# Seven-product pairs of a split-precision feed-forward: the seeding copy behind the previous pair's last products, the sides' sums made during the output projection, the memory statistics one tile later

## The chip, the cores and the metric

One core of one Trainium2 chip runs the whole kernel in one launch. The metric is the device time in microseconds (us), the median of several executions; lower is better.

## The reference

Two transformer blocks run one behind the other on a sequence of 512 tokens of width 1024, in float32. Only the feed-forward of the first block and the start of the second block matter here:

```python
def first_block(x, ...):
    ...
        h = h + merged @ w_out[l]
        u = rms_norm(h, norm_ffn_g[l])
        g, up = jnp.split(u @ w_gate_up[l], 2, axis=-1)
        h = h + (jax.nn.silu(g) * up) @ w_down[l]
    return rms_norm(h, norm_final_g)

def second_block(x, mem, ...):
        h = rmsnorm(x, g_mix_pre[l])
        ...
        mkv = rmsnorm(mem, g_mem[l]) @ w_mem_kv[l]
```

The hidden width of the feed-forward is 2816, 22 tiles of 128 features for the gate and 22 for the up half. `mem` has 256 rows.

## The kernel before

Activations lie feature-major: eight tiles of 128 features by 512 tokens. Float32 operands are split into a high and a low part, and a product is three matmuls (high by high, high by low, low by high), all recorded at L231. For the weights the split is ACT's cast at L358 (`whi`) and DVE's subtraction at L359 (`wlo`), into six buffers. TensorE (PE) accumulates in banks of 512 float32 per partition; a bank's tiles are called `pd`, `ps` and `po` in the profile. An ordinary tile of a product is `fm`: 24 matmuls of 512 columns.

The feed-forward of block 1 (`ffn`, called with the name f1) goes over the hidden features in three parts of 8, 7 and 7 tiles. A part computes its gate and up tiles, applies silu(gate) * up, and then runs the eight `f1_dn` tiles of the down projection over the part's features; the result is added to `h`.

Of the 22 gate/up pairs one is computed the ordinary way, and 21 by a scheme with seven products of half-size blocks in place of eight (`seven`, seven pairs per part). One pair is a 2 x 2 block product: (gate, up weights; two halves of the 1024 features) times (two halves of the features; two halves of the tokens). Each of the products is 12 matmuls of 256 columns. The moving sides `11`, `21` and `22` are slices of the normalised input u; `t1` to `t4` are sums of such slices, kept as `Yh`, `V` (features' tiles 0 and 1) and `Yl`, `K` (tiles 2 and 3). `seven_prep` makes them in four steps: each step scales two tiles on ACT, makes four sums on DVE (L428 to L431) in one buffer `M`, casts 1024 columns on ACT (L535) and subtracts 1024 on DVE (L536).

The results of pair j live in two halves of one `ps` bank (g0, c0) and in a half of the one bank `po` (g1). The halves of `po` alternate with j. Product 11 goes into g0; ACT copies g0 into g1 (the seeding copy, L457); then t3 goes into c0, t2 onto g1, 21 onto g0, t1 onto g1, 22 onto g1, t4 onto c0. ACT copies g1 out twice on the way (L463 and L466), and DVE adds c0 to these copies (L468 and L473). The order on PE is written out by hand (`self.strict` chains the matmuls), a pair's head being put ahead of the last two products of the pair before, q being the pair and last the one before it:

```python
            head(q)
            if last is not None:
                tail(last)
            mid(q)
```

So PE's order is 11(q), 22(last), t4(last), t3(q), t2(q), 21(q), t1(q). The evacuation `ev_7` stands behind `tail`: DVE multiplies g0 and g1 with the norm's row factor R (L1292, L1293), ACT takes the silu (L180), DVE multiplies the up half with R (L1295), multiplies the two (L1296), and the split L535/L536 makes the part's `Ba`/`Bb` and `Ca`/`Cb`.

A framework's scheduler sets each engine's order from the order in which the program issues and from its own estimates. `done_tile` is called behind every tile: it runs the queued `hooks` (two statistics steps of a norm: `cols`, `rows`) and counts down the entries of `self.later`, running those that reach zero. Before, the four steps of `seven_prep` stand in `later` with counts 1, 1, 2, 2, so that they are issued behind the first and second tile of f1 (the gate and up tile of the ordinary pair). `part_hook` runs ahead of part 2's down tiles and issues loading the memory (`mem_load`, tile `Y`), a change of ACT's table (L169), and `mem_stats`: the memory's split (`Yh`, `Yl`), its squares on ACT, their sums on DVE (L595) and two statistics hooks.

Of the kernel before, what the change touches and what calls it, by code (L numbers as in the profile page):

```python
# [9 lines left out]
F32R = mybir.dt.float32r  # L10
# [7 lines left out]
P = 128  # L18
# [27 lines left out]
def weight_plan():  # L46
# [51 lines left out]
    for g in range(2):  # L98
        fm("gb", w, rg(4616 + 512 * g, 512))
        fm("pb", "w_proj_b", rg(512 * g, 512), kt=4)  # L100
    fm("wo", "w_out", rg(0, D))
    ffn("f1", "w_gate_up", "w_down")
    m = "w_mem_kv_2"
    fm("mk", m, rg(0, 512))
# [17 lines left out]
    for g in range(2):  # L122
        fm("ga2", w, rg(4168 + 512 * g, 512))
        fm("ua", "w_up_a_2", rg(512 * g, 512), kt=4)
    fm("wo2", "w_out_2", rg(0, D))
    ffn("f2", "w_ffn_in_2", "w_ffn_out_2")
    return plan

# [18 lines left out]
class Build:  # L147
# [290 lines left out]
    def seven(self, name, x, pairs, evac):  # L438

        nc = self.nc

        def product(ps, b, start=False):
            hi, lo = x[b]
            kw = dict(skip_group_check=True)
            for k, (wh, wl) in enumerate(self.next_half(name)):
                self.mm(ps, wh, hi(k), start=start and k == 0, stop=False, **kw)
                self.mm(ps, wh, lo(k), start=False, stop=False, **kw)
                self.mm(ps, wl, hi(k), start=False, stop=k == 3, **kw)  # L450

        def head(q):
            b = self.bk_s()
            q["g0"], q["c0"] = b[:, 0:256], b[:, 256:512]
            q["g1"] = self.seeded[:, 256 * (q["j"] % 2):256 * (q["j"] % 2) + 256]
            product(q["g0"], "11", True)
            nc.scalar.copy(q["g1"], q["g0"])  # L457

        def mid(q):
            q["u2"], q["u4"] = self.t("s7", [P, 256], F32, bufs=2), self.t("s7b", [P, 256], F32, bufs=1)  # L460
            product(q["c0"], "t3")
            product(q["g1"], "t2")
            nc.scalar.copy(q["u2"], q["g1"])  # L463
            product(q["g0"], "21")
            product(q["g1"], "t1")
            nc.scalar.copy(q["u4"], q["g1"])  # L466
            q["lin"] = self.tmp()
            nc.vector.tensor_add(q["lin"][:, 256:512], q["u4"], q["c0"])  # L468

        def tail(q):  # L470
            product(q["g1"], "22")
            product(q["c0"], "t4")
            nc.vector.tensor_add(q["lin"][:, 0:256], q["u2"], q["c0"])  # L473
            self.done_tile(lambda: evac(q["j"], q["g0"], q["g1"], q["lin"]))

        self.strict = "start"
        last = None
        for j in pairs:
            q = dict(j=j)
# [4 lines that stand above are left out]
            last = q  # L484
        if last is not None:
            tail(last)
        self.strict = None
# [771 lines left out]
    def ffn(self, name, u, st, down_evac, part_hook=None, halves=None, x7=None):  # L1259
        nc = self.nc  # L1260
        uh, ul = u
        rh, rl = self.acc_k(uh), self.acc_k(ul)
        f0 = 0
        for p, n in enumerate(FF_PARTS):
            ah, al = self.pair_tiles("Ba", "Bb"), self.pair_tiles("Ca", "Cb")
            sil = {}

            full = slice(0, S)

            def ev_g(ps, j, w=full):  # L1270
                a = self.tmp()[:, w]
                nc.vector.tensor_mul(a, ps, st["R"][:, w])
                self.last_silu = self.act(a, a, AF.Silu).ins
                sil[j, w.start] = a

            def ev_u(ps, j, w=full):
                b = self.tmp()[:, w]
                nc.vector.tensor_mul(b, ps, st["R"][:, w])
                a = sil.pop((j, w.start))
                nc.vector.tensor_mul(a, a, b)  # L1280
                self.split_to(ah(j)[:, w], al(j)[:, w], a)

            j0 = 0
            if halves is not None and p == 0:
                j0 = NUP // 2
                self.fm_halves(name + "_up", NUP, rh, rl, lambda ps, i, w: (ev_u if i % 2 else ev_g)(ps, i // 2, w),
                               halves)
                self.strict = None

            def ev_7(j, g0, g1, lin):  # L1290
                a = self.tmp()
                nc.vector.tensor_mul(a[:, 0:256], g0, st["R"][:, 0:256])  # L1292
                nc.vector.tensor_mul(a[:, 256:512], g1, st["R"][:, 256:512])  # L1293
                self.last_silu = self.act(a, a, AF.Silu).ins
                nc.vector.tensor_mul(lin, lin, st["R"])  # L1295
                nc.vector.scalar_tensor_tensor(a, lin, -1.0, a, op0=ALU.mult, op1=ALU.mult)  # L1296
                self.split_to(ah(j), al(j), a)

            j7 = n if name not in SEVEN else min(max(SEVEN[name] - f0, j0), n)
            for j in range(j0, j7):  # L1300
                self.fm(name + "_up", rh, rl, lambda ps, j=j: ev_g(ps, j))
                self.fm(name + "_up", rh, rl, lambda ps, j=j: ev_u(ps, j))
            self.seven(name + "_7", x7, range(j7, n), ev_7)
            f0 += n
            if part_hook is not None:
                part_hook(p)
            k0 = KD - NDN if halves is not None and p == 2 else KD
            for k in range(k0):
                self.fm(name + "_dn", ah, al, lambda ps, k=k: down_evac(ps, k, p, full))
            if k0 < KD:  # L1310
                self.fm_halves(name + "_dn", NDN, ah, al, lambda ps, i, w: down_evac(ps, k0 + i, p, w))


    def block1(self):
        nc = self.nc
        x = self.x
        u = uh, ul = self.new_u()
# [28 lines left out]
        q = lambda h: qt_[:, h, :]  # L1346
# [83 lines left out]
        h = self.h = self.t("H16", [P, KD, S])  # L1430
        for k in range(0, KD, 2):
            nc.sync.dma_start(h[:, k:k + 2, :], self.ins["xT"][:, k:k + 2, :])
        u = uh, ul = self.new_u()
        acc = self.t("A", [P, S], F32, bufs=2)

        def ev_wo(ps, k):
            nc.vector.tensor_add(h[:, k, :], h[:, k, :], ps)
            self.split_to(uh[:, k, :], ul[:, k, :], h[:, k, :], self.vec("norm_ffn_g", k))
            self.sq_add(acc, h[:, k, :], k == 0)

        for k in range(KD):
            self.fm("wo", *mp["m"], lambda ps, k=k: ev_wo(ps, k))
        st, self.hooks = self.stat_hooks(acc, "f")

        nx = {}

# [11 lines left out]
        def part_hook(p):  # L1458
            if p == 2:
                self.mem_load()  # L1460
                self.load_lnexp(self.last_silu)
                self.mem_stats()

        th = [self.t(tag, [P, 2, 4, 256], F32R) for tag in ("Yh", "Yl")]
        tl = [self.t(tag, [P, 2, 4, 256], F32R) for tag in ("V8", "K8")]
        x7, steps = self.seven_prep(u, lambda k: th[k // 2][:, k % 2], lambda k: tl[k // 2][:, k % 2],
                                    lambda k: h[:, k, :], lambda k: self.vec("norm_ffn_g", k))
        self.later = [[1 + k // 2, f] for k, f in enumerate(steps)]
        self.deep = True
        self.ffn("f1", u, st, ev_dn, part_hook, x7=x7)  # L1470
        self.deep = False
        return nx
# [373 lines left out]
```

## Time and profile before

| | us |
|---|---|
| median of 3 runs | 1770.49 (1768.11 to 1770.69) |
| the profiled execution | 1770.61 |
| its span in the profile | 1768.0 |
| PE busy | 1720.7 (97%) |
| DVE busy | 1124.5 (64%) |
| ACT busy | 869.0 (49%) |
| POOL busy | 153.5 (9%) |
| share of PE in the chain that ended last | 92% |

The span runs from the first to the last instruction of the profiled execution; the execution's own time is 2.6 us longer. A timeline row reads: start in us from the span's start, duration, engine, line, operation, tile written <- tiles read, count, and in brackets the engine's idle time ahead of the row and what ended it. The end of a matmul is modelled; the spacing of the starts of neighbouring matmuls tells how long one occupies PE. `PEclk` is TensorE's granted clock as a share of the full 2.4 GHz.

### The profile page before, as it was taken

The page shows a single profiled execution, that of the slowest core. Times are in us where ns is not written, and L with a number is a line of the kernel's source. Part 1 is how long each engine was busy: PE and PEld are TensorE (multiplying, and loading weights), DVE is VectorE, ACT ScalarE, POOL GpSimd, SP SyncE. Part 2 cuts the span into 40 slices and gives each one's busy share as a digit, 9 for nine tenths or more (in the row PEclk, how much of TensorE's full clock was granted, in tenths as well). Part 3 has the DMA queues.
Part 4 walks back from the last instruction along what each step waited for, and adds up shares of the span by engine and source line. Part 5 has one row for each costly group of instructions (what it writes and reads, how often), then busy time and mean ns, then how long its engine had stood idle before and what let it go on. Part 6 is the DMA issues. An engine that isn't in the chain of part 4 may idle for free.

```text
span 1768.0 us, 25895 instructions
## 1 busy us (share of the span) xinstructions
PE 1720.7 (97%) x9601; PEld 1446.7 (82%) x9601; DVE 1124.5 (64%) x2363; ACT 869.0 (49%) x1767; POOL 153.5 (9%) x203
## 2 busy tenths in 40 slices
PE   9999999998999999999999999999999999999997
PEld 8878788886988888979989876777779988888887
DVE  5887664567765856777499964666655743344454
ACT  5755655445543534564455567644544533332331
POOL 1400011000100101000000222200000500000001
PEclk9999999998999999999999999999999999999999
DMA  5434215342654645335324211323223233333331
GB/s 181 118 95 120 72 60 162 106 155 78 157 142 120 165 127 137 86 95 179 102 72 108 72 60 59 100 93 118 71 99 120 72 94 95 89 94 94 96 113 54
DMA packets 65661, 187.04 MB, mean 106 GB/s; under 512 B 7840, under 2 KB 10440, under 8 KB 65280
## 3 DMA queue, kind: packets, MB, share of 16 engines
q1 hardware_dynamic: 59456, 174.33, 31.7%
q0 software_dynamic: 6080, 11.08, 3.8%
q8 instruction: 75, 1.23, 0.3%
q14 instruction: 50, 0.41, 0.1%
HBM read 174.87 MB, written 6.84 MB: 103 GB/s over the span
## 4 chain that ended last, share of the span: by engine, by line
PE 92%; DVE 3%; ACT 2%; issue 1%; DMA 1%; POOL 0%; SPq 0%; DVEq 0%; ACTq 0%
PE pd L231 66%; PE ps L231 6%; PE po L231 5%; PE po L795 2%; PE pd L522 2%; PE pd L524 2%; PE pd L523 2%; PE ps L572 1%; PE ps L573 1%; PE ps L785 1%; PE po L1194 1%; DVE ul L539 1%; DMA raw<-in_wts 0%; ACT po L457 0%; PE ps L1160 0%
## 5 line engine op out<-in xcount | busy, mean ns | idle before, releaser
L358 ACT CAST whi<-raw 128x512 fp32r<-128x512 f32 (+3 forms) x536 | 308.7, 582 | 521.3 <-PE pd L231 392.3
L359 DVE TENSOR_TENSOR wlo<-raw,whi 128x512 fp32r<-128x512 f32 (+3 forms) x536 | 346.3, 651 | 244.0 <-ACT whi L358 235.3
L231 PE MATMUL pd<-uh,whi 128*128 128x512 f32 (+1 forms) x1032 | 406.3, 394 | 0.0
L231 PE MATMUL pd<-uh,wlo 128*128 128x512 f32 (+1 forms) x1032 | 404.9, 393 | 0.0
L231 PE MATMUL pd<-ul,whi 128*128 128x512 f32 (+1 forms) x1032 | 404.1, 392 | 0.0
L231 PEld LDWEIGHTS pd<-uh,wlo 128*128 128x128 f32 x1032 | 194.0, 188 | 43.8 <-issue 2.0
L231 PEld LDWEIGHTS pd<-ul,whi 128*128 128x128 f32 x1032 | 193.8, 188 | 41.9 <-issue 2.4
L231 PEld LDWEIGHTS pd<-uh,whi 128*128 128x128 f32 x1032 | 194.0, 188 | 41.0 <-issue 2.5
L231 PE MATMUL pd<-Ba,whi 128*128 128x512 f32 (+1 forms) x240 | 91.6, 382 | 0.0
L231 PE MATMUL pd<-Ca,whi 128*128 128x512 f32 (+1 forms) x240 | 90.9, 379 | 0.0
L231 PE MATMUL pd<-Ba,wlo 128*128 128x512 f32 (+1 forms) x240 | 90.8, 378 | 0.0
L231 PE MATMUL pd<-Bb,whi 128*128 128x512 f32 (+1 forms) x210 | 78.3, 380 | 3.1 <-ACT Bb L535 3.1
L231 PE MATMUL pd<-Bb,wlo 128*128 128x512 f32 (+1 forms) x210 | 80.5, 383 | 0.0
L231 PE MATMUL pd<-Cb,whi 128*128 128x512 f32 (+1 forms) x210 | 80.5, 383 | 0.0
L231 PE MATMUL pd<-Yh,whi 128*128 128x512 f32 (+1 forms) x192 | 72.7, 383 | 0.9 <-DVE H L751 0.9
L231 PE MATMUL pd<-Yl,whi 128*128 128x512 f32 (+1 forms) x192 | 72.4, 377 | 0.0
L231 PE MATMUL pd<-Yh,wlo 128*128 128x512 f32 (+1 forms) x192 | 72.2, 376 | 0.0
L524 PE MATMUL pd<-whi,ul 128*128 128x260 f32 (+1 forms) x232 | 64.8, 286 | 1.5 <-DVE ul L539 1.5
L522 PE MATMUL pd<-whi,uh 128*128 128x260 f32 (+1 forms) x232 | 65.8, 288 | 0.2 <-ACT uh L180 0.2
L523 PE MATMUL pd<-wlo,uh 128*128 128x260 f32 (+1 forms) x232 | 65.2, 283 | 0.0
L231 PEld LDWEIGHTS pd<-Ba,whi 128*128 128x128 f32 x240 | 45.2, 188 | 9.5 <-DVE H L1448 0.6
L231 PEld LDWEIGHTS pd<-Ba,wlo 128*128 128x128 f32 x240 | 45.1, 188 | 9.3
(525 smaller groups left out, 3696.8 us busy)
## 6 DMA issues: line engine op xcount, KB each, us to landing
raw<-in_wts SPq DMA_DIRECT2D x218, 512.0 KB, 3.6
raw<-in_wts SPq DMA_DIRECT2D x32, 448.0 KB, 3.3
PT<-in_wts SPq DMA_DIRECT2D x42, 256.0 KB, 4.2
PT<-in_wts POOLq DMA_DIRECT2D x42, 256.0 KB, 4.7
P<-in_wts SPq DMA_DIRECT2D x21, 256.0 KB, 3.6
raw<-in_wts SPq DMA_DIRECT2D x8, 520.0 KB, 3.4
tabd<-tab SPq DMA_DIRECT2D x8, 320.0 KB, 5.8
H<-in_xT SPq DMA_DIRECT2D x8, 256.0 KB, 6.3
```

The source lines that it names most:

```text
L231: return self.pe(self.nc.tensor.matmul(*args, **kw))
L358: self.nc.scalar.copy(hi, r)
L359: self.nc.vector.tensor_sub(lo, r, hi.bitcast(F32))
L522: mm(pss[i][:, :w], xh[:, kk, sl], hi, start=(kk == 0), stop=False)
L523: mm(pss[i][:, :w], xh[:, kk, sl], lo, start=False, stop=False)
L524: mm(pss[i][:, :w], xl[:, kk, sl], hi, start=False, stop=(kk == 7))
L539: nc.vector.scalar_tensor_tensor(lo, src, g, hi.bitcast(F32), op0=ALU.mult, op1=ALU.subtract)
L572: mm(out, q, khi, start=True, stop=False)
L573: mm(out, q, klo, start=False, stop=True)
L785: nc.tensor.transpose(ps[:, kt * P:(kt + 1) * P], Pt[:, kt * P:(kt + 1) * P], self.ident)
L795: nc.tensor.matmul(o[64 * hh:64 * hh + 64, qt * P:(qt + 1) * P], v[:, kt, h * 64:(h + 1) * 64], PTs[hh][:, kt * P:(kt + 1) * P], start=(kt ...
L1194: nc.tensor.matmul(o[c][64 * hh:64 * hh + 64, kt * P:], bv[:, kt, h * 64:(h + 1) * 64], us[hh]["a"][:, :N], start=False, stop=True, skip_g ...
```

## The change

Four things are done.

1. The seeding copy moves from the end of `head` to the start of `mid`, so that it is issued behind the last two products of the pair before (it is L459 now).
2. The evacuation is cut in two. `ev_7g` (DVE's products of g0 and g1 with R, now L1294 and L1295, and the silu) is issued between products 22 and t4; `ev_7` (the up half, L1300 and L1301, and the split, now L537/L538) behind t4. `done_tile` has nothing left to evacuate.
3. `seven_prep` is called ahead of the loop over the output projection's tiles (`wo`). Steps 0 and 1 are issued behind its tiles 5 and 6; steps 2 and 3 behind the first tile of f1 (counts 0 and 0).
4. `mem_stats` leaves `part_hook` and is issued behind the first down tile of part 2.

```diff
--- before.py
+++ after.py
@@ -454,9 +454,9 @@
             q["g0"], q["c0"] = b[:, 0:256], b[:, 256:512]
             q["g1"] = self.seeded[:, 256 * (q["j"] % 2):256 * (q["j"] % 2) + 256]
             product(q["g0"], "11", True)
+
+        def mid(q):
             nc.scalar.copy(q["g1"], q["g0"])
-
-        def mid(q):
             q["u2"], q["u4"] = self.t("s7", [P, 256], F32, bufs=2), self.t("s7b", [P, 256], F32, bufs=1)
             product(q["c0"], "t3")
             product(q["g1"], "t2")
@@ -469,9 +469,11 @@
 
         def tail(q):
             product(q["g1"], "22")
+            gate = evac[0](q["g0"], q["g1"])
             product(q["c0"], "t4")
             nc.vector.tensor_add(q["lin"][:, 0:256], q["u2"], q["c0"])
-            self.done_tile(lambda: evac(q["j"], q["g0"], q["g1"], q["lin"]))
+            evac[1](q["j"], gate, q["lin"])
+            self.done_tile(lambda: None)
 
         self.strict = "start"
         last = None
@@ -1287,11 +1289,14 @@
                                halves)
                 self.strict = None
 
-            def ev_7(j, g0, g1, lin):
+            def ev_7g(g0, g1):
                 a = self.tmp()
                 nc.vector.tensor_mul(a[:, 0:256], g0, st["R"][:, 0:256])
                 nc.vector.tensor_mul(a[:, 256:512], g1, st["R"][:, 256:512])
                 self.last_silu = self.act(a, a, AF.Silu).ins
+                return a
+
+            def ev_7(j, a, lin):
                 nc.vector.tensor_mul(lin, lin, st["R"])
                 nc.vector.scalar_tensor_tensor(a, lin, -1.0, a, op0=ALU.mult, op1=ALU.mult)
                 self.split_to(ah(j), al(j), a)
@@ -1300,7 +1305,7 @@
             for j in range(j0, j7):
                 self.fm(name + "_up", rh, rl, lambda ps, j=j: ev_g(ps, j))
                 self.fm(name + "_up", rh, rl, lambda ps, j=j: ev_u(ps, j))
-            self.seven(name + "_7", x7, range(j7, n), ev_7)
+            self.seven(name + "_7", x7, range(j7, n), (ev_7g, ev_7))
             f0 += n
             if part_hook is not None:
                 part_hook(p)
@@ -1438,9 +1443,16 @@
             self.split_to(uh[:, k, :], ul[:, k, :], h[:, k, :], self.vec("norm_ffn_g", k))
             self.sq_add(acc, h[:, k, :], k == 0)
 
+        th = [self.t(tag, [P, 2, 4, 256], F32R) for tag in ("Yh", "Yl")]
+        tl = [self.t(tag, [P, 2, 4, 256], F32R) for tag in ("V8", "K8")]
+        x7, steps = self.seven_prep(u, lambda k: th[k // 2][:, k % 2], lambda k: tl[k // 2][:, k % 2],
+                                    lambda k: h[:, k, :], lambda k: self.vec("norm_ffn_g", k))
         for k in range(KD):
             self.fm("wo", *mp["m"], lambda ps, k=k: ev_wo(ps, k))
+            if k in (5, 6):
+                steps[k - 5]()
         st, self.hooks = self.stat_hooks(acc, "f")
+        self.later = [[0, steps[2]], [0, steps[3]]]
 
         nx = {}
 
@@ -1459,13 +1471,8 @@
             if p == 2:
                 self.mem_load()
                 self.load_lnexp(self.last_silu)
-                self.mem_stats()
-
-        th = [self.t(tag, [P, 2, 4, 256], F32R) for tag in ("Yh", "Yl")]
-        tl = [self.t(tag, [P, 2, 4, 256], F32R) for tag in ("V8", "K8")]
-        x7, steps = self.seven_prep(u, lambda k: th[k // 2][:, k % 2], lambda k: tl[k // 2][:, k % 2],
-                                    lambda k: h[:, k, :], lambda k: self.vec("norm_ffn_g", k))
-        self.later = [[1 + k // 2, f] for k, f in enumerate(steps)]
+                self.later = [[1, self.mem_stats]]
+
         self.deep = True
         self.ffn("f1", u, st, ev_dn, part_hook, x7=x7)
         self.deep = False
```

Three places of the order that results are shown.

ACT around the seeding copy of the second pair of part 0; `whi` are weight casts, `tmp` the silu, `s7b` the copy at L466. Before:

```order
L466 COPY s7b_4592<-po_4389 128x256
L358 CAST whi_4683<-PT_4395 128x512
L457 COPY po_4389<-ps_4665 128x256
L358 CAST whi_4709<-raw_4572 128x512
L358 CAST whi_4736<-T_4738 128x512
L180 ACTIVATE tmp_4726<-tmp_4726 128x512
L358 CAST whi_4754<-P_4397 128x512
```

With the change:

```order
L466 COPY s7b_4592<-po_4055 128x256
L358 CAST whi_4682<-PT_4417 128x512
L358 CAST whi_4712<-raw_4572 128x512
L180 ACTIVATE tmp_4698<-tmp_4698 128x512
L459 COPY po_4055<-ps_4665 128x256
L358 CAST whi_4736<-T_4738 128x512
L358 CAST whi_4754<-P_4419 128x512
```

The copy stood ahead of the cast of `raw`; it now stands behind the silu of the pair before, which stands two casts earlier than it did.

PE at the change from product t4 of the first pair (into `ps_4559`) to t3 of the second (into `ps_4665`); the bracket names the engine whose semaphore a row waits for. Before:

```order
L231 MATMUL ps_4559<-Yl_4386,whi_4611 128x256
L231 MATMUL ps_4559<-K_1023_4388,whi_4611 128x256
L231 MATMUL ps_4559<-Yl_4386,wlo_4612 128x256
L231 MATMUL ps_4665<-Yh_4385,whi_4628 128x256
L231 MATMUL ps_4665<-V_1022_4387,whi_4628 128x256
```

With the change:

```order
L231 MATMUL ps_4559<-Yl_4052,whi_4611 128x256
L231 MATMUL ps_4559<-K_965_4054,whi_4611 128x256
L231 MATMUL ps_4559<-Yl_4052,wlo_4612 128x256
L231 MATMUL ps_4665<-Yh_4051,whi_4628 128x256 [waits Activation_49]
L231 MATMUL ps_4665<-V_964_4053,whi_4628 128x256
```

The first matmul of t3 has a wait for ACT that it did not have. The instruction on ACT that it waits for is the copy L459.

ACT in the first pair of part 0, up to the last step of `seven_prep`; `R` is the norm's row factor, the casts to `Yl` belong to steps 2 and 3. Before:

```order
L642 COPY R_4527<-ps_4522 128x512
L180 ACTIVATE tmp_4537<-H_958_4043,vecs_65 128x512
L180 ACTIVATE tmp_4538<-H_958_4043,vecs_65 128x512
L358 CAST whi_4593<-T_4595 128x512
L457 COPY po_4389<-ps_4559 128x256
L180 ACT_TABLE_LOAD
L180 ACTIVATE tmp_4529<-tmp_4529 128x512
L180 ACTIVATE tmp_4548<-H_958_4043,vecs_65 128x512
L535 CAST Yl_4386<-M_1067_4541 128x1024
L180 ACTIVATE tmp_4549<-H_958_4043,vecs_65 128x512
L535 CAST Ba_4391<-tmp_4529 128x512
L535 CAST Yl_4386<-M_1070_4552 128x1024
```

With the change:

```order
L537 CAST Yl_4052<-M_1057_4491 128x1024
L358 CAST whi_4574<-raw_4443 128x512
L644 COPY R_4549<-ps_4544 128x512
L358 CAST whi_4593<-T_4595 128x512
L459 COPY po_4055<-ps_4559 128x256
L180 ACT_TABLE_LOAD
L180 ACTIVATE tmp_4551<-tmp_4551 128x512
L537 CAST Ba_4413<-tmp_4551 128x512
L537 CAST Yl_4052<-M_1060_4502 128x1024
```

All four scaling copies (`tmp<-H`) have moved ahead of this stretch, and step 2's cast too; step 3's cast stands behind the first silu and the cast of `Ba`. On DVE step 3's last two sums stand behind the product of the silu and the up half (L1282) and, between them, a sum of weights (L322).

Behind part 2's last pair, ACT's order was: `Yh` (8), a cast, two squares, the silu, the table load, a cast, a square, the cast of `Bb`. It is now: the silu, the table load, `Yh` (8), a cast, the cast of `Bb`; the seven squares into `tmp` stand ahead of the silu, behind the copy L466. Ahead of the down matmuls that wait for `Bb` PE now has the memory's two statistics matmuls and its two broadcasts.

## Rows read from the trace of the kernel before

**Rows 1.** The page: busy time of each engine (us, share of the span, instructions).

```profile
PE 1720.7 (97%) x9601; PEld 1446.7 (82%) x9601; DVE 1124.5 (64%) x2363; ACT 869.0 (49%) x1767; POOL 153.5 (9%) x203
```

**Rows 2.** PE's waits from 424 to 777 us: us in total, times, longest us.

```profile
PE po L231 <- ACT po L457: 16.2, 18, 0.9
PE ps L231 <- ACT Yl L535: 4.9, 2, 2.5
PE pd L231 <- ACT Bb L535: 3.1, 1, 3.1
PE ps L231 <- ACT po L457: 3.0, 3, 1.3
PE ps L231 <- DVE K L536: 1.4, 2, 0.7
```

**Rows 3.** Timeline of PE, one steady pair: start, us, ..., [idle before <-releaser].

```profile
489.09 0.28 PE L231 MATMUL ps<-uh,wlo 128*128 128x256 f32 x1
490.28 0.39 PE L231 MATMUL po<-uh,whi 128*128 128x256 f32 x1 [0.91 <-ACT po L457]
490.50 0.28 PE L231 MATMUL po<-ul,whi 128*128 128x256 f32 x1
...
491.80 0.28 PE L231 MATMUL ps<-Yh,whi 128*128 128x256 f32 x1
...
493.22 0.28 PE L231 MATMUL ps<-Yh,whi 128*128 128x256 f32 x1
```

**Rows 4.** Timeline of ACT in the same pair.

```profile
489.86 0.37 ACT L457 COPY po<-ps 128x256 f32<-128x256 f32 x1
...
494.21 0.63 ACT L180 ACTIVATE tmp<-tmp 128x512 f32<-128x512 f32 x1 [0.29 <-DVE tmp L1292]
494.75 0.60 ACT L358 CAST whi<-P 128x512 fp32r<-128x512 f32 x1
```

**Rows 5.** Timeline of DVE in the same pair.

```profile
489.99 0.69 DVE L359 TENSOR_TENSOR wlo<-PT,whi 128x512 fp32r<-128x512 f32 x1 [0.37 <-ACT whi L358]
492.06 0.42 DVE L1293 TENSOR_TENSOR tmp<-po,R 128x256 f32<-128x256 f32 x1 [1.39 <-PE po L231]
```

**Rows 6.** Timeline of PE, first pair of part 0.

```profile
428.00 0.39 PE L231 MATMUL ps<-Yh,whi 128*128 128x256 f32 x1 [1.27 <-ACT po L457]
...
437.75 0.41 PE L231 MATMUL po<-Yh,whi 128*128 128x256 f32 x1
```

**Rows 7.** Timeline of ACT, first pair of part 0.

```profile
429.26 0.63 ACT L180 ACTIVATE tmp<-tmp 128x512 f32<-128x512 f32 x1
...
430.41 1.03 ACT L535 CAST Yl<-M 128x1024 fp32r<-128x1024 f32 x1
```

**Rows 8.** Timeline of DVE, first pair of part 0.

```profile
429.92 0.69 DVE L1280 TENSOR_TENSOR tmp<-tmp,tmp 128x512 f32<-128x512 f32 x1 [0.72 <-ACT tmp L180]
...
431.47 1.23 DVE L536 TENSOR_TENSOR K<-M,Yl 128x1024 fp32r<-128x1024 f32 x1 [0.25 <-ACT Yl L535]
```

**Rows 9.** Stretches: length; PE, PEld, DVE, ACT, POOL busy (instructions); PEclk, DMA share, GB/s.

```profile
431.40:435.80 4.40, 1.38 (x3) 0.79 (x3) 3.26 (x6) 2.18 (x4) 0.00 (x0) 0.50 0.00 0
445.00:760.00 315.00, 297.10 (x2084) 275.06 (x2085) 212.84 (x370) 144.45 (x275) 30.38 (x35) 1.00 0.51 133
767.70:772.00 4.30, 4.21 (x11) 3.12 (x12) 4.09 (x11) 3.52 (x9) 0.00 (x0) 0.61 0.17 68
```

**Rows 10.** Timeline of PE, behind part 2's last pair.

```profile
767.79 0.97 PE L231 MATMUL pd<-Bb,whi 128*128 128x512 f32 x3 [3.06 <-ACT Bb L535]
```

**Rows 11.** Timeline of ACT, behind part 2's last pair.

```profile
763.75 0.72 ACT L180 ACTIVATE tmp<-Y 128x256 f32<-128x256 f32 x2
...
766.30 0.62 ACT L358 CAST whi<-raw 128x512 fp32r<-128x512 f32 x1
766.82 0.41 ACT L180 ACTIVATE tmp<-Y 128x256 f32<-128x256 f32 x1
767.14 0.60 ACT L535 CAST Bb<-tmp 128x512 fp32r<-128x512 f32 x1
```

## The prediction

> **What bounds the kernel now.** Read the page first: PE is busy 97% of the span [rows 1]. So only a time in which PE stands still, or runs at the lower clock, can be won, and work taken from ACT or DVE counts where PE waits for it. The next view is therefore the list of PE's waits over the stretch that the change touches, from the first pair to the first down tiles of part 2 [rows 2]. It has three kinds. Eighteen times PE waits 0.9 us for the seeding copy, 16.2 us in all: 21 pairs less the first of each part, which has no pair ahead of it and waits at another place (the 3.0 us on `ps`). In the first pair of part 0 it waits for the sums of the moving sides (4.9 us for `Yl`, 1.4 for `K`). Behind the last pair of part 2 it waits 3.1 us for `Bb`. Then the timelines say what one such wait costs and what released it. I take the three in turn.
>
> **Part 1 and 2: the seeding copy and the split evacuation.** First the price of today's wait. The last matmul of product 11 starts at 489.09 and the first of 22 at 490.28; t4 to t3 is 1.42 us for 12 matmuls, a pitch of 0.118 [rows 3]. So 1.19 - 0.118 = 1.07 us are lost, and the first matmul behind the wait is followed after 0.22 in place of 0.118, another 0.10: 1.17 us a pair. (The 0.91 that the row prints is smaller because the matmul's modelled end, 0.28 after its start, is taken as busy.) The copy needs only 0.37 of it [rows 4]; the rest is its place behind a weight cast.
>
> With the change 22 starts behind 11 at once, since what it adds onto was copied in the pair before. What is late next is t3: it now waits for the copy, as the order shows. It writes c0, the copy reads g0, the other half of the same bank. That such a wait is real the trace shows in the first pair: t3 waits 1.27 us there for the same copy of the other half [rows 6], and in the steady pair 22 waits for a copy into the other half of `po` [rows 3].
>
> The Trainium skill, "PSUM — Partial Sum Buffer", section "PSUM bank collisions raise a hardware error", says that two engines have to be kept apart by bank and group of partitions even where their addresses differ, and that the tools add a dependency for it. By that rule the sum is the one that follows (14.8); for one who goes by addresses t3 would be free and the sum would be that of the first rival (21.1). The two rows named above bear the rule out.
>
> So I place the copy from the start of t4, called T. DVE's product with g1 starts at T + 0.26 today and takes 0.42 [rows 3, 5]. A silu starts 0.03 behind the end of the product that it needs (494.18 to 494.21), and the next instruction on ACT 0.54 behind the silu's start [rows 4]. So the silu starts at T + 0.71, the copy at T + 1.25, and it ends at T + 1.62. PE resumed 0.05 behind the copy's end before (490.23 to 490.28) [rows 3, 4]: t3 at T + 1.67, where t4 alone would let it start at T + 1.42. A wait of 0.25 and the 0.10 behind it: 0.35 us a pair. Gain 1.17 - 0.35 = 0.82, by 18 pairs **14.8 us**.
>
> The bounds: t3 not held at all gives 18 x 1.17 = 21.1; the copy a full 0.82 later than I place it gives 0. I take the middle since each link is a row of the same pair. The three pairs that open a part keep their wait.
>
> Two covers have to hold. DVE must reach g1's product at T + 0.26: ahead of it stands a subtraction of 0.69 that starts at 489.99 today [rows 5] and hangs on a cast on ACT, which does not move. 22 now ends earlier: T becomes 490.28 + 1.52 - 1.17 = 490.63 on the same scale, so the product is wanted at 490.89, and the subtraction ends at 490.68. It holds by 0.2 us. And t4, which writes the other half of the bank that g0's product reads, is safe as that product stands ahead of the subtraction. The weights' transfers have the same bytes in some 7% less time; DMA's share is 0.51 over these 315 us, DVE is busy 213 of them and ACT 144 [rows 9], so none becomes the bound on the average.
>
> **Part 3: the sums of the moving sides.** Today the two `Yl` waits and the two `K` waits stand between t3's first matmul at 428.00 and t2's at 437.75 [rows 2, 6]. Now steps 0 to 2 are through before the first pair, and only step 3 is late. Its chain by rows: the wait of t3 began at 428.00 - 1.27 = 426.73, and the copy takes 0.37 and 0.05, so t3 cannot start before 427.15; without the two scaling copies ahead of it I put it at 427.55, in the middle to today's 428.00. The silu starts 1.31 behind the copy's end (427.95 to 429.26, ACT's table is loaded between) [rows 6, 7], so at 428.8; it takes 0.63, DVE's product behind it 0.69 [rows 7, 8], and then come a sum of 256 columns, a sum of weights and the last sum, 0.42, 0.69 and 0.42 by their sizes [rows 5, 8]: 431.7, or 431.5 as neighbours overlap a little. The cast to `Yl` takes 1.03 and `K` 1.23 [rows 7, 8]: 433.8. Behind it stand two or three matmuls at the lower clock, some 0.6 us: t2 at 434.4 in place of 437.75. Gain **3.3 us**. Bounds: nothing (step 3 kept as late as it was), and, where no sum is late at all, 437.75 less 427.55 less the 1.42 of t3, 8.8. The two steps that moved into the output projection cost ACT and DVE there what they cost before; PE is covered by full tiles of 24 matmuls, and I take nothing for it.
>
> During these waits the granted clock is 0.50, the lower of the two levels (1.2 GHz) [rows 9]; since one wait of about 3 us stays, I keep that loss.
>
> **Part 4: the memory's statistics.** PE resumes at 767.79 after 3.06 us of waiting for the cast of `Bb` [rows 10]. On ACT two squares, a weight cast and a square stand ahead of that cast; they take 0.72 as a pair, 0.52 and 0.32 by their starts [rows 11]. All three have moved out of the chain, the squares into time in which ACT idled: **1.5 us**, with 0 as the bound below (the cast could wait for DVE instead) and the whole 3.06 above. After the wait the granted clock is 0.61 and eleven matmuls of 512 columns keep PE busy for 4.21 us [rows 9]; at twice the pitch of 0.118 they would take 2.6. With 1.6 us of waiting, and in it the statistics' four small matmuls, I expect the clock to stay up, as it does at 1.00 through the eighteen waits of 0.9 us [rows 9]: another **1.6 us**. If it falls all the same the part brings 1.5.
>
> The sum: 14.8 + 3.3 + 1.5 + 1.6 = 21.2 us from the profiled execution's 1770.6, so 1749.4; the median of the runs lies 0.1 lower, so **1749.3**.
>
> **The rivals.** 0.2% is 3.5 us, about what a measurement of this kernel can tell from no change.
>
> First, *the copy is hidden wholly*: t3 doesn't wait, or the silu is quicker. 21.1 + 6.4 = 27.5, the time 1743. For it: only 0.25 us are missing. Against: the order's new wait, and both rows above.
>
> Second, *the wait moves and keeps most of its size*: the copy stands behind the silu, the silu behind DVE, and all behind 22. If it is held some 0.5 us longer than I place it, by a weight cast or a subtraction that lands in between (0.52 to 0.69 each), a pair gains 0.3 and the whole is 5.4 + 6.4 = 11.8, the time 1758.5. For it: the cover on DVE is 0.2 us. Against: DVE idles 1.39 us ahead of that product today [rows 5].
>
> Third, and on the other side, *DVE falls behind*: its work for one pair is the same, in a period 0.8 us shorter. If g1's product comes behind two subtractions more (2 x 0.69 = 1.4 us), the copy ends at T + 3.0, t3 loses 1.6 and 0.1, and a pair loses 1.75 where it lost 1.17: eighteen pairs lose 10.4, the other parts' 6.4 come off, and the time is 1774.4. That is the point from which it decides, slower by over 0.2%: a product with g1 1.4 us later than I place it; where parts 3 and 4 bring nothing, 1.0 us does. DVE's 213 of 315 us speak against a lasting backlog.
>
> Fourth, *the change doesn't do what it says in part 3 or 4*: step 3 stays as late, the clock falls as before; 14.8 + 1.5, the time 1754. The scheduler has also turned some rows round in block 2; PE is full there, so I give it 2 us either way and no sign.
>
> **How the numbers follow.** Forecast 0.56 (1746 to 1752.5: two us for the reordering and the bounds of parts 3 and 4), wholly hidden 0.12 (1743), parts 3 or 4 void 0.12 (1754), wait kept 0.12 (1758.5), DVE behind 0.08 (1766 to 1780, some 0.03 of it beyond 1774). The range that leaves about 2 in 10 out goes from 1743 to 1758: half of the first rival, half of the second and the third lie beyond. Faster by over 0.2% (below 1767): the first four and a little of the fifth, 0.93; within 0.2%: 0.04; slower: 0.03.
>
> **What would show it.** Right: no wait for the copy in front of 22; eighteen waits of about 0.25 us (or, as the row prints with the modelled end, near 0.1) in front of t3, released by ACT L459; a pair's period of about 10.25 us; one `Yl` wait in place of two; a wait for `Bb` under 1.7 us with a granted clock near 1.00 behind it. Wrong: t3 waiting over 0.6 us, the product with g1 starting later than 0.5 us behind t4's start, PE waiting for the row factor's broadcast around 424 us, or new waits in block 2.

## The result and the profile after

The changed kernel takes 1746.93 us (median of 4 runs, 1745.97 to 1748.1) against 1769.99 for the kernel before, 0.9872 of its time (95% interval 0.9855 to 0.9889): 23.1 us less, where 21.2 were forecast. The profiled execution has a span of 1744.3 us against 1768.0, 23.7 less; the places below are read from it.

The page of the changed kernel, busy times as in [rows 1]: PE does the same work in 2.8 us less, and is busy for 98% of a shorter span.

```profile
PE 1717.9 (98%) x9601; PEld 1446.7 (83%) x9601; DVE 1128.6 (65%) x2363; ACT 871.2 (50%) x1767; POOL 152.6 (9%) x203
```

PE's waits from 395 to 777 us, the view of [rows 2] (total, times, longest). The eighteen waits in front of 22 are gone, one `Yl` wait is left of two and it is longer, and `Bb` is 0.7 in place of 3.1. The three waits for the copy are those of the pairs that open a part. The new waits of t3 in the other eighteen pairs are not in this list, though they are there: see the next fence.

```profile
PE ps L231 <- ACT Yl L537: 3.7, 1, 3.7
PE ps L231 <- ACT po L459: 2.6, 3, 0.9
PE ps L231 <- DVE K L538: 0.8, 1, 0.8
PE pd L231 <- ACT Bb L537: 0.7, 1, 0.7
```

Timeline of PE in the steady pair that [rows 3] show (t4 of the pair before starts at 484.50, its last matmul at 485.81, t3 at 486.12; the last row is the next pair's t4).

```profile
484.50 0.28 PE L231 MATMUL ps<-Yh,whi 128*128 128x256 f32 x1
...
485.81 0.28 PE L231 MATMUL ps<-Yl,wlo 128*128 128x256 f32 x1
486.12 0.39 PE L231 MATMUL ps<-Yh,whi 128*128 128x256 f32 x1
486.35 0.28 PE L231 MATMUL ps<-V,whi 128*128 128x256 f32 x1
...
494.68 0.28 PE L231 MATMUL ps<-Yh,whi 128*128 128x256 f32 x1
```

t3 starts 0.31 behind t4's last matmul where the pitch is 0.12: 0.19 of waiting, and 0.11 more ahead of the second matmul. That is 0.30 us a pair against 1.17 before, and a period of 10.18 us (10.2 to 10.3 in the other steady pairs). The row prints no wait because the last matmul's modelled end lies at 486.09: the spacing of the starts tells it, the list of waits does not.

What holds t3 is on ACT and DVE, the views of [rows 4, 5]:

```profile
484.63 0.62 ACT L358 CAST whi<-raw 128x512 fp32r<-128x512 f32 x1 [0.79 <-PE po L231]
485.16 0.63 ACT L180 ACTIVATE tmp<-tmp 128x512 f32<-128x512 f32 x1
485.70 0.37 ACT L459 COPY po<-ps 128x256 f32<-128x256 f32 x1
```

```profile
484.70 0.42 DVE L1295 TENSOR_TENSOR tmp<-po,R 128x256 f32<-128x256 f32 x1
```

DVE's product with g1 (L1295) starts 0.20 behind t4's start, the silu at 0.66, the copy at 1.20; it ends at 1.57, and t3 starts at 1.62. ACT comes to the silu straight from the cast of `raw`, 0.53 behind that cast's start, and DVE's product ends 0.04 ahead of the silu: two things let the silu go at the same time.

The first pair of part 0, the view of [rows 6]:

```profile
427.32 0.39 PE L231 MATMUL ps<-Yh,whi 128*128 128x256 f32 x1 [0.86 <-ACT po L459]
...
432.34 0.49 PE L231 MATMUL ps<-Yl,whi 128*128 128x256 f32 x1 [3.69 <-ACT Yl L537]
433.60 0.58 PE L231 MATMUL ps<-K,whi 128*128 128x256 f32 x1 [0.77 <-DVE K L538]
...
434.19 0.41 PE L231 MATMUL po<-Yh,whi 128*128 128x256 f32 x1
```

Three stretches, columns as in [rows 9]: the first two follow that wait, the third follows the wait for `Bb`.

```profile
433.00:437.00 4.00, 3.40 (x16) 3.40 (x17) 1.24 (x2) 0.80 (x2) 0.00 (x0) 0.50 0.04 16
437.00:440.00 3.00, 3.00 (x18) 3.00 (x18) 0.69 (x1) 1.32 (x3) 0.00 (x0) 0.62 0.43 105
747.70:752.00 4.30, 4.26 (x17) 3.02 (x18) 4.08 (x8) 3.09 (x7) 0.00 (x0) 1.00 0.46 122
```

And behind part 2's last pair, the views of [rows 10, 11]:

```profile
747.74 0.97 PE L231 MATMUL pd<-Bb,whi 128*128 128x512 f32 x3 [0.67 <-ACT Bb L537]
```

```profile
741.51 0.63 ACT L180 ACTIVATE tmp<-tmp 128x512 f32<-128x512 f32 x1
742.16 1.28 ACT L169 ACT_TABLE_LOAD   x1
743.45 3.31 ACT L180 ACTIVATE Yh<-Y,vecs 128x256 fp32r<-128x256 f32 x8
...
747.07 0.61 ACT L537 CAST Bb<-tmp 128x512 fp32r<-128x512 f32 x1
```

The silu, the table load and the eight `Yh` now stand ahead of the cast of `Bb` with no square between; PE resumes after 0.67 us, and the granted clock behind it is 1.00 where it was 0.61.

How far the change is ahead, at the same matmuls of both traces:

| place | before, us | after, us | ahead, us | gained since the row above |
|---|---|---|---|---|
| first pair, product 11 | 425.07 | 424.80 | 0.27 | |
| first pair, t2 | 437.75 | 434.19 | 3.56 | 3.3 |
| second pair, product 11 | 443.42 | 440.74 | 2.68 | -0.9 |
| part 2's last pair, last matmul of t4 | 760.53 | 742.15 | 18.38 | 15.7 |
| a broadcast of block 2's first norm | 815.5 | 793.5 | 22.0 | 3.6 |
| end of the span | 1768.0 | 1744.3 | 23.7 | 1.7 |

The -0.9 of the third row belongs to this execution and not to the order; the run with the statistics put back, below, shows it.

### The profile page after: what moved, and what is told of

The parts are those of the page before. It is cut to its first block, busy times and chain, and to the rows that moved or that the text cites. A ratio compares the mean times of both kernels' runs of the same rounds, so it can differ in the third digit from the quotient of the medians.

```text
span 1744.3 us, 25883 instructions
## 1 busy us (share of the span) xinstructions
PE 1717.9 (98%) x9601; PEld 1446.7 (83%) x9601; DVE 1128.6 (65%) x2363; ACT 871.2 (50%) x1767; POOL 152.6 (9%) x203
## 4 chain that ended last, share of the span: by engine, by line
PE 95%; DVE 2%; ACT 2%; POOL 0%; DMA 0%; issue 0%; SPq 0%; DVEq 0%; ACTq 0%
PE pd L231 67%; PE ps L231 7%; PE po L231 5%; PE po L797 2%; PE pd L524 2%; PE pd L526 2%; PE pd L525 2%; PE ps L574 1%; PE ps L575 1%; PE ps L787 1%; PE po L1196 1%; PE ps L1162 0%; DVE ul L541 0%; PE ps L1167 0%; PE po L973 0%
```

## The experiments

Ten kernels were run, all edits of the changed kernel. Theory A is the prediction's: the place of the copy brings most, t3 keeps a short wait since copy and matmul meet in one bank, step 3 holds the first pair, and deferring the statistics shortens the wait for `Bb`. Its rivals: that the split evacuation and not the copy brings it, that t3 is late for another reason, and that the end's gain is the split's. The kernel before took 1769.6 to 1770.6 us beside the changed kernel and the three groups of these runs, so differences of under 1 us between kernels of different groups say nothing.

**The evacuation whole again.**

```diff
             product(q["g1"], "22")
-            gate = evac[0](q["g0"], q["g1"])
             product(q["c0"], "t4")
             nc.vector.tensor_add(q["lin"][:, 0:256], q["u2"], q["c0"])
-            evac[1](q["j"], gate, q["lin"])
+            evac[1](q["j"], evac[0](q["g0"], q["g1"]), q["lin"])
```

> The evacuation is whole again behind t4; the copy stays behind the previous pair's products. In the order that results the copy stands ahead of the silu and waits only for DVE's product with g1. Theory A (the place of the copy is the whole gain, and the residual wait of t3 comes from the silu that the split put ahead of it): the copy ends some 1.1 us behind t4's start, t3 does not wait, the period of a pair falls from 10.18 to about 9.9 us, and the time falls by 18 x 0.3 = 5.4 us below the changed kernel, to about 1741. Theory B (the split evacuation is needed, because the copy otherwise waits for the late silu or for DVE's late products): t3 waits 1 us or more, the time is 1765 or above.

Measured: 1743.73 us (1743.18 to 1747.39), 0.9851 of before (0.9835 to 0.9868). On ACT the copy now comes ahead of the silu (timeline of one pair; t4 starts at 482.14):

```profile
482.26 0.62 ACT L358 CAST whi<-raw 128x512 fp32r<-128x512 f32 x1 [0.80 <-PE po L231]
482.80 0.36 ACT L459 COPY po<-ps 128x256 f32<-128x256 f32 x1
...
484.55 0.63 ACT L180 ACTIVATE tmp<-tmp 128x512 f32<-128x512 f32 x1 [0.23 <-DVE tmp L1293]
```

It is through 1.02 us behind t4's start, and t3 keeps its pitch: each pair is 0.30 faster than in the changed kernel, and at part 2's last t4 this kernel is 6.5 us ahead of it. Then it gives 4.1 of that back: the span is 2.4 us shorter, the median 3.2. ACT's order behind part 2's last pair is the one of before, with `Yh` and two squares ahead of the silu:

```profile
735.24 3.31 ACT L180 ACTIVATE Yh<-Y,vecs 128x256 fp32r<-128x256 f32 x8 [0.21 <-PE ps L231]
...
738.86 0.72 ACT L180 ACTIVATE tmp<-Y 128x256 f32<-128x256 f32 x2
739.48 0.61 ACT L180 ACTIVATE tmp<-tmp 128x512 f32<-128x512 f32 x1
...
742.25 0.60 ACT L536 CAST Bb<-tmp 128x512 fp32r<-128x512 f32 x1
```

PE's wait for `Bb` and the stretch behind it:

```profile
PE pd L231 <- ACT Bb L536: 3.0, 1, 3.0
```

```profile
744.00:748.00 4.00, 4.00 (x11) 3.12 (x11) 3.79 (x9) 3.35 (x7) 0.00 (x0) 0.58 0.16 20
```

The wait for `Bb` is 3.0 us again and the clock falls again, although the statistics are deferred as in the change. So the copy's place alone brings the pairs' gain (theory A); the split costs 0.3 us a pair, and pays at the end of part 2. That end is what the expected 1741 had left out.

**The split alone, the copy back behind product 11** (the moved line put back into `head`).

> The split evacuation alone: the copy is back behind product 11, the rest is as changed. Theory A: 22 waits 0.9 us for the copy again, eighteen times, t3 does not wait; the time rises by 18 x 0.87 = 15.7 us over the changed kernel, to about 1762.5. Theory B (the earlier silu and products bring part of the gain): it rises by less than 10 us.

Measured: 1762.67 us (1762.43 to 1764.11), 0.9956 (0.994 to 0.9972), 15.7 over the changed kernel. The waits in front of 22 are back as they were:

```profile
PE po L231 <- ACT po L457: 16.2, 18, 0.9
...
PE pd L231 <- ACT Bb L537: 0.7, 1, 0.7
```

Theory A: a steady pair takes 11.1 us again in place of 10.2. And `Bb` stays short, as the split is in.

**The copy tied behind the silu, the evacuation whole**: a copy that comes late, as in the rival on the slower side:

```diff
         def mid(q):
-            nc.scalar.copy(q["g1"], q["g0"])
+            if last is None:
+                nc.scalar.copy(q["g1"], q["g0"])
+            else:
+                with self.tc.issue_after(self.last_silu):
+                    nc.scalar.copy(q["g1"], q["g0"])
```

> The evacuation is whole behind t4 and the copy is tied behind its silu: the rival on the slower side, made on purpose. The silu starts about 2.4 us behind t4's start as in the kernel before, so the copy ends near T + 3.3 and t3 starts near T + 3.4 where 1.42 would be its turn: a loss of about 2.0 + 0.1 us a pair against 0.3 in the changed kernel. If the price of a late copy is one for one, 18 x 1.8 = 32 us over the changed kernel, about 1779, slower than before. If something else absorbs the delay (weights, the order on PE), under 15 us.

Measured: 1807.84 us (1807.17 to 1808.5), 1.0208 (1.0188 to 1.0229). The waits for the copy (L463 here), and three stretches of one pair (t3 starts at 473.56):

```profile
PE ps L231 <- ACT po L463: 32.1, 18, 1.8
```

```profile
470.20:475.00 4.80, 3.02 (x26) 2.81 (x25) 4.32 (x9) 2.74 (x5) 0.36 (x1) 0.99 0.79 198
475.00:478.50 3.50, 3.50 (x19) 3.50 (x18) 1.40 (x3) 1.31 (x4) 0.86 (x1) 0.52 0.23 53
478.50:481.00 2.50, 2.50 (x24) 2.50 (x23) 1.42 (x3) 0.85 (x3) 0.00 (x0) 1.00 0.90 167
```

The wait is as worked out: 1.8 printed, and by the starts t3 is 1.94 us late. But the time is 29 us above the expectation. After the wait the granted clock falls, to 0.52 over 3.5 us of the pair shown, and it does so in 15 of the 18 pairs: a pair that stays at 1.00 takes 11.9 us, one whose clock falls 13.5. That is 24 us; and behind the last pair PE waits 3.0 us for `Bb` again, with the slow matmuls behind it, which makes some 4.7. So the price of a late copy is one for one only while the clock holds, and the slower rival of the prediction reckoned it one for one. Whether the clock would fall at that rival's 1.6 us too, no run shows.

**t3 and t4 in a bank of their own.**

```diff
-            q["g0"], q["c0"] = b[:, 0:256], b[:, 256:512]
+            q["g0"] = b[:, 0:256]
         def mid(q):
+            q["c0"] = self.bk_s()[:, 256:512]
-            product(q["c0"], "t3")
+            product(q["c0"], "t3", True)
```

> As changed, but t3 and t4 go into a half of a bank of their own in place of the other half of the bank that the copy reads; ACT's and DVE's order around the copy is the same. If t3 waits because copy and matmul meet in one bank: the wait on ACT in front of t3 is gone, the period falls from 10.18 to about 9.9 us and the time by about 5 us, to 1742. If t3 is late for another reason (its weights, or the release of a bank), it stays at 10.18 and 1747.

Measured: 1740.19 us (1739.43 to 1741.2), 0.9827 (0.9812 to 0.9842), 6.7 under the changed kernel. PE's waits from 395 to 800 us, all of them:

```profile
PE ps L231 <- ACT Yl L538: 4.8, 1, 4.8
PE ps L231 <- DVE K L539: 0.7, 1, 0.7
PE pd L231 <- ACT Bb L538: 0.7, 1, 0.7
```

The copy still stands behind the silu, and nothing waits for it, not even in the pairs that open a part: sharing the bank is what made t3 wait. (The two halves were also halves of one tile of the program; no run has two tiles in one bank, so which of the two the program's order went by isn't told apart.) The Trainium skill, "PSUM — Partial Sum Buffer", section "PSUM bank collisions raise a hardware error", has the accesses of two engines guarded by bank and not by address; the trace agrees, 0.30 us of waiting a pair with the bank shared and 0 without. What an access without the wait would do, no run here shows. In the first pair what is saved at t3 reappears in the wait for `Yl` (4.8 in place of 3.7): step 3 is what is late there.

**The statistics put back** ahead of part 2's down tiles:

```diff
-                self.later = [[1, self.mem_stats]]
+                self.mem_stats()
```

> As changed, but the memory's statistics are issued ahead of part 2's down tiles again. Theory A (as predicted: deferring them took the squares out of ACT's chain to the cast of Bb): the wait for Bb is back near 3 us, the clock falls behind it, the time rises by some 3.5 us to about 1750.5. Theory B (the split evacuation did it, since with the evacuation whole the wait is 3.0 us though the statistics are deferred): ACT's order at that place stays as changed, the wait stays near 0.7 us and the time near 1747.

Measured: 1747.13 us (1746.34 to 1749.43), 0.9872 (0.9856 to 0.9889), 0.2 from the changed kernel.

```profile
PE pd L231 <- ACT Bb L537: 0.7, 1, 0.7
```

The wait is 0.7, and the order on PE, ACT and DVE is that of the change, not only there but from the first instruction to the last. This edit does nothing: theory B. With the silu issued early, ACT is through with it and with the table load before the eight `Yh`; where it stands behind t4, `Yh` and two squares come first, as in the first of these runs.

With the changed kernel's order throughout, this run also tells how firm the first pair's figures are. From t2 (436.21) to the next product 11 (441.51) it takes 5.30 us, where the changed kernel took 6.55 (434.19 to 440.74). Stretches of both, this kernel first:

```profile
436.20:438.40 2.20, 2.20 (x12) 2.20 (x12) 0.69 (x1) 0.62 (x1) 0.00 (x0) 0.50 0.00 0
438.40:441.50 3.10, 3.10 (x27) 3.10 (x27) 1.31 (x2) 1.51 (x3) 0.00 (x0) 0.98 0.38 103
```

```profile
434.20:439.20 5.00, 5.00 (x25) 5.00 (x25) 1.39 (x2) 1.51 (x3) 0.00 (x0) 0.50 0.18 54
```

The same matmuls behind the same waits, but the lower clock lasts 2.2 us behind t2's start here and 5.0 there. The four other kernels with this order of the first pair take 5.3 to 5.8 us for the stretch: the changed kernel's profiled execution is the odd one.

**The steps put back** into the feed-forward (counts 1, 1, 2, 2 in `later`).

> As changed, but the four steps of the sides' sums stand in the feed-forward again. Expected by the prediction's working: two waits for Yl (2.5 and 2.3 us) in the first pair, the second pair's head about 2.4 us later (what the trace of the change shows of this part), the time near 1749.5. Rival: the steps in the output projection cost there what they save, or the other rows that changed place in block 2 hang on it: within 1 us of 1747.

Measured: 1750.23 us (1749.39 to 1750.87), 0.9886 (0.9871 to 0.9901), 3.3 over the changed kernel. The waits are those of before [rows 2], two for `Yl` and two for `K`:

```profile
PE ps L231 <- ACT Yl L537: 4.9, 2, 2.5
...
PE ps L231 <- DVE K L538: 1.4, 2, 0.7
```

The second pair's head comes 2.5 us later than in the changed kernel's profiled execution, with its long stretch at the lower clock; the medians are 3.3 apart. The part brings about 3 us, and the rival, within 1 us of 1747, is out.

**The steps as early as their inputs**, behind the output projection's tiles 4 to 7:

```diff
-            if k in (5, 6):
-                steps[k - 5]()
+            if k >= 4:
+                steps[k - 4]()
...
-        self.later = [[0, steps[2]], [0, steps[3]]]
```

> As changed, but the four steps stand behind the output projection's tiles 4 to 7, as early as their inputs are there. In the order K's last part stands on DVE ahead of the ordinary pair's evacuation. If step 3's place is what holds t3: no wait for Yl or K in the first pair, no fall of the clock there, t2 some 4.8 us earlier and the lower clock's 0.9 to 2 us back, the time near 1740.5. Rival: ACT and DVE are too full at the end of the output projection, the row factor's broadcast or product 11 wait 2 us or more, and half of that is lost.

Measured: 1741.2 us (1738.44 to 1741.27), 0.9832 (0.9817 to 0.9846), 5.7 under the changed kernel by the medians, 7.8 by the profiled spans (the profiled execution took 1738.4, the three others 1741.2). Timelines of PE and of DVE in the first pair:

```profile
427.49 0.38 PE L231 MATMUL ps<-Yh,whi 128*128 128x256 f32 x1 [0.92 <-ACT po L459]
...
428.89 0.28 PE L231 MATMUL ps<-Yl,wlo 128*128 128x256 f32 x1
429.01 0.28 PE L231 MATMUL po<-Yh,whi 128*128 128x256 f32 x1
```

```profile
426.10 1.23 DVE L538 TENSOR_TENSOR K<-M,Yl 128x1024 fp32r<-128x1024 f32 x1 [0.26 <-ACT Yl L537]
```

`K` is whole at 427.33, before t3 starts. t3 runs through, t2 starts 5.2 us earlier than in the changed kernel, and the second pair's head at 433.28, 7.5 us earlier. From t2 to there it takes 4.27 us, at the full clock: 2.3 less than in the changed kernel's profiled execution, 1.0 less than with the statistics put back. The row factor's broadcast starts at 424.52 against 424.44 in the changed kernel: the output projection had room.

**Early steps and the copy ahead of the silu.** The copy is issued between `ev_7g`'s products and its silu:

```diff
-            def ev_7g(g0, g1):
+            def ev_7g(g0, g1, seed):
...
+                if seed:
+                    seed()
                 self.last_silu = self.act(a, a, AF.Silu).ins
```

> Steps as early as in the kernel of this call that has them behind tiles 4 to 7, and the copy ahead of the silu while the evacuation stays split. If the copy's wait in t3 comes from the silu ahead of it and the short wait for Bb from the split, both are had at once: no wait in t3 in eighteen pairs (a period of 9.9 us), a wait for Bb of some 0.7 us, 18 x 0.3 = 5.4 us below the kernel with early steps, near 1735. Rival: the copy now waits for DVE's product with g1 and lands late, period 10.1 or more.

Measured: 1735.44 us (1733.93 to 1736.41), 0.9802 (0.9787 to 0.9817), 5.8 under the kernel with early steps alone. The copy and the silu of one pair on ACT, t4 starting at 437.68:

```profile
438.34 0.36 ACT L470 COPY po<-ps 128x256 f32<-128x256 f32 x1
438.64 0.63 ACT L180 ACTIVATE tmp<-tmp 128x512 f32<-128x512 f32 x1
```

```profile
PE pd L231 <- ACT Bb L541: 0.7, 1, 0.7
```

Both gains are there at once: no wait in front of t3 in the eighteen pairs (a steady pair takes 9.9 us), a short one for `Bb`.

**Early steps and the own bank**, the two edits above together.

> Steps behind tiles 4 to 7 and t3, t4 in a bank of their own; the copy stays behind the silu. If the two are independent: no wait in front of t3 in any of the 21 pairs (5.4 us for eighteen of them, 0.9 us and the refill for each of the first three where t2 does not wait in its place), near 1733. Rival: t2 then waits for the copy in the first pairs, or the extra bank makes a tile wait: 1735 or above.

Measured: 1730.88 us (1729.45 to 1731.89), 0.9781 (0.9767 to 0.9796): the fastest of all, 16.1 under the changed kernel and 38.7 under the one before. Of PE's waits between 395 and 800 us one is left:

```profile
PE pd L231 <- ACT Bb L538: 0.7, 1, 0.7
```

It gains more over early steps alone than the eighteen pairs (5.4): a pair that opens a part begins without its 0.9 us wait too, 1.0 us each by the starts. That makes 8.5 us, against 8.3 by the profiled spans and 10.3 by the medians.

**The same with the copy ahead of the silu.**

> The same with the copy ahead of the silu. Since t3 waits no longer either way, the copy's place brings nothing more: within 1 us of the kernel with the copy behind the silu. If t2 or 22 waited for the copy there, it is 2 us or more faster.

Measured: 1731.91 us (1730.12 to 1732.57), 0.9789 (0.9773 to 0.9805), 1.0 above the one without, the intervals overlapping. As expected: with a bank of its own for t3 the copy's place on ACT no longer matters.

## Why the prediction was right, and where it was not

The forecast of 1749.3 missed by 2.4 us, inside its range: 1.9 us more were saved than the 21.2 forecast, and 0.5 lies in the median of the kernel before (1770.49 on record, 1769.99 here). By its own steps:

- *The seeding copy, 14.8.* Measured 15.7. The chain from t4's start (T) over DVE's product and the silu to the copy was right link by link: t3 was put at T + 1.67 and starts at T + 1.62. That the weight cast now ahead of the silu ends just as DVE's product does was not in the chain; that it cost nothing is luck. Undoing the copy's move costs 15.7 us, and separating the banks takes the last 0.30 a pair away, so the wait that was forecast for t3 is real and comes from sharing the bank.
- *The cover on DVE.* It held: L1295 starts 0.20 behind t4's start, earlier than the 0.26 that was asked for.
- *The sums of the sides, 3.3.* Up to t2 it was right: 434.4 forecast, 434.19 measured, and one long wait in place of two. For the clock the prediction kept the loss of before. In the profiled execution the loss was larger: t2 to the next product 11 takes 6.55 us, against 5.67 before, so 0.9 of the 3.3 was given back there. But the other five kernels with that order take 5.3 to 5.8, and undoing the part costs 3.3 by the medians. So size and step are borne out within about 1 us; why the lower clock lasts longer in one execution than in another stays open.
- *The memory's statistics, 1.5 + 1.6.* The amount was near, the cause was not. From the last matmul of part 2's last t4 to the first matmul of the statistics shown below the kernel before takes 44.8 us and the changed kernel 41.1: 3.7 us less. PE resumes 1.7 us earlier behind t4 (1.5 forecast); most of the other 2.0 is the clock that stays up, some 1.7 by the 0.61 over 4.3 us of before [rows 9] (1.6 forecast). The prediction gave all this to the deferral. The deferral brings nothing (1747.13 without it), and the split evacuation brings it: that stretch takes 41.0 to 41.1 us in all nine kernels with the split, and 44.8, 44.8 and 45.8 in the three without. The step that failed is "All three have moved out of the chain", put down to part 4, where the order with the change was read without asking which of the edits made it.
- *Block 2, no sign.* The last 1.7 us of the span's difference arise behind the broadcast of block 2's first norm. From there to the end it takes 952.5 us before and 950.8 with the change, but 950.5 to 952.0 in seven other kernels whose order there is that of the change: most of the 1.7 is scatter, and whether anything is left stays open. Such scatter is seen elsewhere too: product 11 of the first pair starts at 424.8 in the changed kernel and at 426.8 with the statistics put back, where the order up to there is the same.

The two ends of that stretch of 44.8 and 41.1 us are the t4 of the table above and these rows, before and after:

```profile
805.29 0.95 PE L1507 MATMUL ps<-ones,A 128*128 128x1 f32 x8
```

```profile
783.21 0.95 PE L1514 MATMUL ps<-ones,A 128*128 128x1 f32 x8
```

Of the rivals, *hidden wholly* needed another bank or another place of the copy, and both could be had. *DVE behind* did not come; a copy made late in another way, behind the silu, cost more than one for one, since the clock falls too. And the split evacuation, which the prediction took together with the copy, is two things: it hurts each pair by putting the silu ahead of the copy while t3 shares the bank, and it helps at the end of part 2.

## What to carry to other kernels

When one edit moves several things, price each from the order that it alone makes: here the split looked like the copy's helper and was its last obstacle, and the deferral that seemed to shorten the end did nothing. Before a wait is shortened, ask whether the two instructions need to meet at all: with a second bank t3 no longer waits, in either order on ACT that was run. And compute the sums that a stage begins with as soon as their inputs are there; here a wait of 3.7 us at the first pair's start cost the waiting and then 1.0 to 2.3 us of slow matmuls behind it. And before a microsecond at the lower clock is explained, look at a second execution with the same order.

## What the runs showed of the hardware

The granted clock falls behind waits shorter than the 2.5 to 3.7 us of the first pair and of `Bb`. In the kernel with the copy tied behind the silu, waits of 1.8 us printed, one in each pair, are followed by the lower clock in 15 of 18 pairs; waits of 0.9 in each pair left it at 1.00 [rows 9], and so does the one of 0.67 for `Bb`. How long the lower clock lasts behind the same waits differs between executions: t2 to the next product 11 took 5.3 to 6.6 us in six kernels with one order. And a wait of PE can be missing from the list of waits: eighteen of 0.19 us are hidden in the modelled end of the matmul ahead, and only the starts show them.
